# Two 64-row fp32 up-projections of a recurrence rewritten as hi/lo split products over 128 rows

## The chip, the cores and the metric

The kernel runs on one core of a Trainium2 chip. The metric is the device time of one execution in microseconds, the median of several runs. A core has a matrix engine (PE, whose weight loads are shown as PEld), a vector engine (DVE), an activation engine (ACT), a general engine (POOL), and DMA queues, of which this kernel issues nearly all from SP. Each engine works through its own list of instructions in order, and semaphores tie the lists together.

## The reference, cut to what matters

One decoder layer at SEQ 1024, D_MODEL 1024: a projection of the normed input, two token mixers beside each other (a recurrence called RWKV-7 and a state-space model called S5), an output projection, and a squared-ReLU MLP. The change touches the decay `w` and the gate `a` of the recurrence, each of which comes from a 64-column low-rank projection:

```python
r, k, v, wd, ad, gd = jnp.split(zm, [W, 2*W, 3*W, 3*W + 64, 3*W + 64 + 64], axis=-1)   # W = 512
w = jnp.exp(-DECAY_SCALE * jax.nn.sigmoid((w0 + jnp.tanh(wd) @ w_decay_up).astype(f32)))  # (64 -> 512)
a = jax.nn.sigmoid(a0 + ad @ w_aaa_up)                                                     # (64 -> 512)
```

Both products contract over 64. `w` and `a` then feed the recurrent state of 8 heads of 64.

## The kernel before, in words

Everything is held transposed: 128 features on the partitions, 512 tokens (one half `h` of the sequence) along the row. Products over weights are done in "split" form: a float32 tensor is written as hi + lo, both in the reduced type fp32r (hi by an ACT copy, lo by a DVE subtraction), and three products replace one, hi x hi, hi x lo and lo x hi (`mmacc`, lines 163 to 165). These are the *split products*; the page prints their operands as f32 too, and they are known by their lines. All other products (lines 183, 176, 549, 550, 588, 606 to 760) take plain float32 operands on PE.

The input projection makes 128 columns (`ct`) at a time: `load_w` brings and splits the weights, `mmacc` does 24 split products into a PSUM tile `mm` (two buffers), `zmix` scales by `rs` (the inverse norm, only known after `x_norm`) and mixes with the shifted tokens. Column 12 holds `wd` and `ad` one above the other; `z_lora` (line 307) makes it for each half into the tile `la`, with a tanh on the upper 64 rows. Column 13 (`sg`) is the gate.

The recurrence is cut into four rounds of two *units* (a unit is a pair of heads `hp` in a half `h`): `prep` (line 537, run 8 times) loads the unit's columns back from DRAM and calls the two products of this case, line 549 (`pw`, decay) from rows 0 to 63 of `lora` and `la`, and line 550 (`pa`) from rows 64 to 127. Each is a 64 x 128 weight against 64 x 512. Tile `swp` and tile `a` come from them. Then follow products within chunks of 64 tokens (`gram1`, `gram2`), a triangular inverse, a solve, and `sweep` (line 724): eight chunk steps, in each of which line 735 makes the next state `psn`, ACT writes it to `St` (lines 738, 123), and line 741 the output, for both units in turn. `post` ends the unit. S5 (`s5`) and the rest follow.

Up to the MLP the order of each engine's list is set by a scheduler that plays the program through with its own table of costs and takes what is ready by priority; the recurrence has high priority, and the input projection's split products fill in. From the MLP on the order is written by hand.

At the start, `raw` holds the eight 128 x 512 pieces of the input's first half in eight tiles that later steps use again: piece 3 is in the buffer tagged `kmod`, which `x_norm(1)` then uses for piece 3 of the second half, and `prep` for its tile `kmod`. `x_norm(h)` squares on ACT, adds into `xacc` on DVE, sums over partitions on PE (line 183, tile `stat`), scales on DVE (line 114, `statm`), takes the power on POOL, and goes by ACT and PE (line 176) into `rs`, without which no column can leave PSUM.

Of the kernel before, what the change touches and what calls it, by code (L numbers as in the profile page):

```python
# [9 lines left out]
F32 = mybir.dt.float32  # L10
F32R = mybir.dt.float32r
I32 = mybir.dt.int32
AF = mybir.ActivationFunctionType
# [61 lines left out]
def trunk(ctx, tc, A):  # L75
    nc = tc.nc
    PE, V, S, G, SY = nc.tensor, nc.vector, nc.scalar, nc.gpsimd, nc.sync

    def pool(name, bufs=1, space=None, c=None, **kw):
        if space is not None:  # L80
            kw["space"] = space
        return (c or ctx).enter_context(tc.tile_pool(name=name, bufs=bufs, **kw))
# [13 lines left out]
    def K(n):  # L96
        o, w = CST[n]
        return cst[:, o:o + w] if o < KEPT else cstw[:, o - KEPT:o - KEPT + w]

    def P(n, i):  # L100
        o, w = COL[n]
        return col[:, o + i:o + i + 1]
# [7 lines left out]
    def ts(e, out, in0, s1, op0, s2=None, op1=None):  # L110
        if op1 is None:
            e.tensor_scalar(out=out, in0=in0, scalar1=s1, scalar2=None, op0=op0)
        else:
            e.tensor_scalar(out=out, in0=in0, scalar1=s1, scalar2=s2, op0=op0, op1=op1)  # L114

    def tt(out, a, b, op):
        V.tensor_tensor(out=out, in0=a, in1=b, op=op)  # L117

    def stt(out, a, s, b, op0, op1):
        V.scalar_tensor_tensor(out=out, in0=a, scalar=s, in1=b, op0=op0, op1=op1)  # L120

    def act(out, in_, f, **kw):
        S.activation(out=out, in_=in_, func=f, **kw)  # L123

    M_, A_, B_ = ALU.mult, ALU.add, ALU.subtract
# [41 lines left out]
    def mmtile(p, tag="mm"):  # L167
        return p.tile([128, 512], F32, tag=tag, name=tag)
# [37 lines left out]
    wz = pool("wz", 2)  # L206

    w2 = pool("w2", 2, None, win)
# [3 lines left out]
    w0 = pool("w0", 1, None, ready, side="right")  # L212
# [10 lines left out]
    def st(shape=(128, 512)):  # L223
        return ps_st.tile(list(shape), F32, tag="st", name="st")
# [59 lines left out]
    def zcol(ct, h):  # L284
        x = xg[h]
        w = early.pop(ct) if ct in early else load_w(A["w_in"][ct], 1024)
        p = sm() if ct in (12, 13) and h == 0 else mmtile(ps_mm)
        mmacc(p, w, 8, lambda k: x[k][:, 0], lambda k: x[k][:, 1])
        return p

    def zmix(ct, h, out, p=None):
        p = p or zcol(ct, h)
        if normed[0]:
            act(out, p, AF.Copy, scale=omu[:, ct:ct + 1])
            stt(out[:, 1:512], p[:, 0:511], P("mu", ct), out[:, 1:512], M_, A_)
            stt(out[:, 0:1], carry[:, ct:ct + 1], P("mu", ct), out[:, 0:1], M_, A_)
            return
        z = wz.tile([128, 513], F32, tag="z", name="z")
        tt(z[:, 1:513], p, rs[h], M_)
        G.memset(z[:, 0:1], 0.0)  # L300
        G.tensor_copy(out=carry[:, ct:ct + 1], in_=z[:, 512:513])
        act(out, z[:, 1:513], AF.Copy, scale=omu[:, ct:ct + 1])
        stt(out, z[:, 0:512], P("mu", ct), out, M_, A_)

    la, sg = {}, {}

    def z_lora(h):
        la[h] = w2.tile([128, 512], F32, tag="la", name="la")
        p12, p13 = (first.pop(0), first.pop(0)) if first else (None, None)
        zmix(12, h, la[h], p12)  # L310
        act(la[h][0:64], la[h][0:64], AF.Tanh)
        sg[h] = w2.tile([128, 512], F32, tag="sg", name="sg")
        zmix(13, h, sg[h], p13)
        act(sg[h], sg[h], AF.Tanh, scale=0.5)
        ts(V, sg[h], sg[h], 0.5, M_, 0.5, A_)
# [33 lines left out]
    x_norm(0, raw)  # L349
    cstw = w1.tile([128, NCST - KEPT], F32, name="cstw")  # L350
    SY.dma_start(out=cstw, in_=A["cst"][:, KEPT:NCST])
    lora = w0.tile([128, 512], F32, name="lora")
    SY.dma_start(out=lora, in_=A["lora"])
    wgate = w1.tile([128, 512], F32, name="wgate")
    SY.dma_start(out=wgate, in_=A["wgate"])

# [180 lines left out]
    def prep(hp, h, slot):  # L537
# [8 lines left out]
        cs = slice(hp * 128, hp * 128 + 128)  # L546
        B, abd, rbd, BK = Bt[slot], abds[slot], rbds[slot], BKs[slot]
        pw, pa = st(), st()
        PE.matmul(pw, lhsT=lora[0:64, cs], rhs=la[h][0:64], start=True, stop=True)
        PE.matmul(pa, lhsT=lora[64:128, cs], rhs=la[h][64:128], start=True, stop=True)  # L550
        G.memset(swp[:, :, 0:1], 0.0)
        act(swp[:, :, 1:65], c8(pw), AF.Tanh, scale=0.5, bias=hw0[:, hp:hp + 1])
        act(swp[:, :, 1:65], swp[:, :, 1:65], AF.Copy, scale=0.5, bias=0.5)
# [344 lines left out]
    def rw_open(i):  # L898
        pr, h = pairs[i]
        with tc.high_priority():  # L900
            units[i] = [prep(2 * pr + n, h, n) for n in range(2)]
# [21 lines left out]
    def zprep(h):  # L923
        if h:
            xg[h] = make_xg(h, s2)
        z_lora(h)
# [67 lines left out]
    for m in range(8):  # L994
        if m % 2 == 0:
            w = load_w(A["w_proj"][m // 2], 1024)
        for h in range(2):
            p = mmtile(ps2, "b")
# [19 lines left out]
    for m in range(8):  # L1018
        w = load_w(A["w_glu"][m], 1024)
        for h in range(2):  # L1020
            pa, pb = mmtile(ps2, "b"), mmtile(ps2, "b")
# [9 lines left out]
            hi, lo = t[:, 0], t[:, 1]  # L1031
# [92 lines left out]
    for i, m in enumerate((0, 4, 1, 5, 2, 6, 3, 7)):  # L1124
# [7 lines left out]
        for h in range(2):  # L1132
            x = xs[m][:, h]
            p = mmtile(ps2, "b")
# [193 lines left out]
    def norm_step(i):  # L1328
# [5 lines left out]
        if i == 6:  # L1334
# [6 lines left out]
            pair[1].take("P2")  # L1341

    prep(2)
    prep(3)
    prep(4)
    ahead, stats = 5, []
    for i, (j, n) in enumerate(steps):
        r, o = divmod(i, 14)
# [129 lines left out]
    lo, hi = (0, 256), (256, 512)  # L1478
# [82 lines left out]
```

## Time and profile before

| | |
|---|---|
| median of 3 runs | 1520.98 us (1516.17 to 1527.92) |
| the profiled execution, its own time | 1516.6 us |
| its span from the first to the last instruction | 1514.8 us |
| PE busy | 1487.8 us, 98% of the span |
| DVE busy, ACT busy | 1076.9 us (71%), 728.4 us (48%) |
| granted clock of PE | 0.997 of full speed (2.4 GHz) |

The profile has a page (engines, time slices, the chain of work that ended last, groups of instructions) and views of its trace: stretches of time, waits, a timeline, and all instructions of a tile. A matmul's printed duration includes the part that overlaps with the next one; what one costs in a row of them is the distance between starts.

### The profile page before, as it was taken

What the parts mean: (1) busy time and instruction counts of PE and PEld (TensorE: products, weight loads), DVE (VectorE), ACT (ScalarE), POOL (GpSimd) and SP (SyncE); (2) the same over time, 40 slices, a digit from 0 to 9 for tenths busy, and PEclk for the clock granted to TensorE, in tenths of its full rate; (3) what the DMA queues carried; (4) which work ended last, traced back from release to release, by engine and by line L of the source; (5) the groups of instructions that cost most, each with busy time, mean ns of one, the idle gap of its engine ahead of it and who ended that gap; (6) DMA issues with size and microseconds to landing.
All of it is one profiled execution on the core that took longest, in us unless ns stands there. A gap on an engine that the chain in (4) does not pass through costs nothing.

```text
span 1514.8 us, 22409 instructions
## 1 busy us (share of the span) xinstructions
PE 1487.8 (98%) x8056; PEld 1216.2 (80%) x8056; DVE 1076.9 (71%) x2119; ACT 728.4 (48%) x1260; POOL 79.9 (5%) x108
## 2 busy tenths in 40 slices
PE   7999999999999999999999999999999999999996
PEld 5788887878788877878888888888888788888885
DVE  8669768888558768764656667777777767777574
ACT  6654766756656453323444454444444543333441
POOL 3110001101002001000000000000000000000000
PEclk9999999999999999999999999999999999999999
DMA  7554533444423525574114424444444686455571
GB/s 240 180 158 142 162 93 113 124 125 134 132 79 102 186 63 158 165 248 141 56 56 141 172 84 160 153 153 147 158 151 180 240 296 224 161 190 182 189 250 56
DMA packets 137679, 232.74 MB, mean 154 GB/s; under 512 B 42528, under 2 KB 52896, under 8 KB 137568
## 3 DMA queue, kind: packets, MB, share of 16 engines
q1 hardware_dynamic: 135776, 225.02, 45.2%
q10 hardware_dynamic: 1152, 4.19, 0.8%
q0 software_dynamic: 640, 2.10, 0.6%
q8 instruction: 64, 1.05, 0.3%
q14 instruction: 47, 0.39, 0.1%
HBM read 167.16 MB, written 62.91 MB: 152 GB/s over the span
## 4 chain that ended last, share of the span: by engine, by line
PE 88%; DVE 4%; ACT 3%; DMA 2%; issue 2%; SPq 0%; POOL 0%; POOLq 0%; DVEq 0%; ACTq 0%
PE mm L165 7%; PE mm L163 7%; PE mm L164 7%; PE b L163 5%; PE b L165 5%; PE b L164 5%; PE b L1385 4%; PE b L1386 4%; PE b L1387 4%; PE mm L1116 4%; PE mm L1117 4%; PE mm L1118 4%; PE b L1116 2%; PE b L1117 2%; PE b L1118 2%; PE sm L721 2%
## 5 line engine op out<-in xcount | busy, mean ns | idle before, releaser
L163 PE MATMUL mm<-s,whi 128*128 128x512 f32 x528 | 212.5, 402 | 0.0
L165 PE MATMUL mm<-s,wlo 128*128 128x512 f32 x528 | 212.1, 402 | 0.0
L164 PE MATMUL mm<-s,whi 128*128 128x512 f32 x528 | 209.6, 397 | 0.0
L123 ACT ACTIVATE whi<-wraw 128x512 fp32r<-128x512 f32 x176 | 103.2, 624 | 150.9 <-PE mm L164 58.6
L117 DVE TENSOR_TENSOR wlo<-wraw,whi 128x512 fp32r<-128x512 f32 x176 | 116.6, 684 | 49.1 <-ACT whi L123 45.0
L123 ACT ACTIVATE gp<-s 128x512 fp32r<-128x512 f32 (+1 forms) x127 | 81.7, 653 | 119.3 <-DVE s L117 102.5
L117 DVE TENSOR_TENSOR gp<-s,gp 128x512 fp32r<-128x512 f32 (+1 forms) x127 | 91.3, 722 | 55.3 <-ACT gp L123 55.2
L165 PEld LDWEIGHTS mm<-s,wlo 128*128 128x128 f32 x528 | 99.3, 188 | 23.8 <-issue 4.0
L163 PEld LDWEIGHTS mm<-s,whi 128*128 128x128 f32 x528 | 99.3, 188 | 23.8 <-issue 4.1
L164 PEld LDWEIGHTS mm<-s,whi 128*128 128x128 f32 x528 | 99.3, 188 | 22.8 <-issue 3.6
L1385 PE MATMUL b<-gp 128*128 128x512 f32 (+1 forms) x272 | 103.5, 380 | 2.1 <-DVE row L117 2.1
L1386 PE MATMUL b<-gp 128*128 128x512 f32 (+1 forms) x272 | 103.0, 379 | 0.0
L1387 PE MATMUL b<-gp 128*128 128x512 f32 (+1 forms) x272 | 102.9, 378 | 0.0
L123 ACT ACTIVATE gp<-kx 128x1024 fp32r<-128x1024 f32 x40 | 42.4, 1060 | 120.6 <-DVE kx L117 76.8
L186 POOL TENSOR_TENSOR statm<-statm,cst 128x8 f32<-128x8 f32 (+2 forms) x23 | 36.3, 1581 | 1066.6 <-DVE statm L114 994.1
L117 DVE TENSOR_TENSOR gp<-kx,gp 128x1024 fp32r<-128x1024 f32 x40 | 49.0, 1225 | 54.5 <-ACT gp L123 54.5
L117 DVE TENSOR_TENSOR s<-s,s 128x512 f32<-128x512 f32 (+2 forms) x120 | 75.4, 650 | 5.0 <-ACT s L823 4.6
L1116 PE MATMUL mm<-kx,gp 128*128 128x512 f32 x192 | 74.8, 389 | 0.0
L1118 PE MATMUL mm<-kx,gp 128*128 128x512 f32 x192 | 74.7, 389 | 0.0
L1117 PE MATMUL mm<-kx,gp 128*128 128x512 f32 x192 | 74.7, 389 | 0.0
L123 ACT ACTIVATE row<-row 128x512 f32<-128x512 f32 x64 | 40.0, 627 | 55.4 <-DVE row L120 55.4
L1385 PEld LDWEIGHTS b<-gp 128*128 128x128 f32 x272 | 51.6, 190 | 12.0 <-DVE row L117 2.5
(355 smaller groups left out, 3579.6 us busy)
## 6 DMA issues: line engine op xcount, KB each, us to landing
wraw<-in_w_in SPq DMA_DIRECT2D x136, 256.0 KB
wblk<-in_w_dn SPq DMA_DIRECT2D x40, 512.0 KB
s<-in_w_up SPq DMA_DIRECT2D x32, 512.0 KB
traw<-tDT SPq DMA_DIRECT2D x32, 512.0 KB
tD<-row SPq DMA_DIRECT2D x48, 256.0 KB
tDT<-gp SPq DMA_DIRECT2D x42, 256.0 KB
xraw<-in_xT SPq DMA_DIRECT2D x32, 256.0 KB
gD<-gt SPq DMA_DIRECT2D x32, 256.0 KB
```

What stands on the lines that cost most here:

```text
L117: V.tensor_tensor(out=out, in0=a, in1=b, op=op)
L123: S.activation(out=out, in_=in_, func=f, **kw)
L163: PE.matmul(out, lhsT=hi[:, a], rhs=rhi(k), start=(k == 0), stop=False)
L164: PE.matmul(out, lhsT=hi[:, a], rhs=rlo(k), start=False, stop=False)
L165: PE.matmul(out, lhsT=lo[:, a], rhs=rhi(k), start=False, stop=(k == nk - 1))
L186: G.tensor_tensor(out=m, in0=m, in1=K("mhalf")[:, 0:nj * n].rearrange("p (a b) -> p a b", b=n), op=ALU.pow)
L1116: PE.matmul(p, lhsT=hi[:, a], rhs=bh, start=(first and k == 0), stop=False, skip_group_check=True)
L1117: PE.matmul(p, lhsT=hi[:, a], rhs=bl, start=False, stop=False, skip_group_check=True)
L1118: r = PE.matmul(p, lhsT=lo[:, a], rhs=bh, start=False, stop=(k == 3), skip_group_check=True)
L1385: PE.matmul(p, lhsT=wh[:, a], rhs=th[:, c], start=first, stop=False, skip_group_check=True)
L1386: PE.matmul(p, lhsT=wh[:, a], rhs=tl[:, c], start=False, stop=False, skip_group_check=True)
L1387: PE.matmul(p, lhsT=wl[:, a], rhs=th[:, c], start=False, stop=stop, skip_group_check=True)
```

## The change

The tile `la` becomes two tiles of 128 rows, `dw` and `da`, each with hi on the 64 rows where the value stood and lo on the other 64. The weight tile `lora` becomes four tiles, `dwhi`, `dwlo`, `dahi`, `dalo`: the hi tile has hi of the weight on both halves, the lo tile has lo of the weight on the half of hi and zeros on the other. Two split products then give hi x (hi + lo) and lo x hi. So 16 products become 32 of another type. The weights' raw tile `lraw` takes the buffer tagged `kmod`, and the input's raw tile `lain` one of the two buffers tagged `zo`, through which all columns of `z_hp` pass.

```diff
     def z_lora(h):
-        la[h] = w2.tile([128, 512], F32, tag="la", name="la")
         p12, p13 = (first.pop(0), first.pop(0)) if first else (None, None)
-        zmix(12, h, la[h], p12)
-        act(la[h][0:64], la[h][0:64], AF.Tanh)
+        x = wz.tile([128, 512], F32, tag="zo", name="lain")
+        zmix(12, h, x, p12)
+        act(x[0:64], x[0:64], AF.Tanh)
+        dw, da = [w2.tile([128, 512], F32R, tag=n, name=n) for n in ("dw", "da")]
+        act(dw[0:64], x[0:64], AF.Copy)
+        act(da[64:128], x[64:128], AF.Copy)
+        tt(dw[64:128], x[0:64], dw[0:64].bitcast(F32), B_)
+        tt(da[0:64], x[64:128], da[64:128].bitcast(F32), B_)
+        la[h] = dw, da
...
-    lora = w0.tile([128, 512], F32, name="lora")
-    SY.dma_start(out=lora, in_=A["lora"])
+    lraw = w0.tile([128, 512], F32, tag="kmod", name="lraw")
+    SY.dma_start(out=lraw, in_=A["lora"])
+    lora = {}
+    for n, q, o in (("dw", slice(0, 64), slice(64, 128)), ("da", slice(64, 128), slice(0, 64))):
+        hi, lo = [w0.tile([128, 512], F32R, name=f"{n}{x}") for x in ("hi", "lo")]
+        act(hi[q], lraw[q], AF.Copy)
+        act(hi[o], lraw[q], AF.Copy)
+        act(lo[o], K("ones")[o].to_broadcast([64, 512]), AF.Copy, scale=0.0)
+        tt(lo[q], lraw[q], hi[q].bitcast(F32), B_)
+        lora[n] = hi, lo
...
-        PE.matmul(pw, lhsT=lora[0:64, cs], rhs=la[h][0:64], start=True, stop=True)
-        PE.matmul(pa, lhsT=lora[64:128, cs], rhs=la[h][64:128], start=True, stop=True)
+        for p, n, x in ((pw, "dw", la[h][0]), (pa, "da", la[h][1])):
+            hi, lo = lora[n]
+            PE.matmul(p, lhsT=hi[:, cs], rhs=x, start=True, stop=False)
+            PE.matmul(p, lhsT=lo[:, cs], rhs=x, start=False, stop=True)
```

The new products are lines 567 and 568 of the changed kernel; lines behind `prep` are 18 higher there (735 is 753). The scheduler deals all lists anew up to the MLP.

On PE, the second half's first unit. In the list before, its two products stand alone among the split products of the input projection (`mm`):

```order
L163 MATMUL mm<-s_2604,whi 128x512
L549 MATMUL st<-la,lora 128x512
L164 MATMUL mm<-s_2604,whi 128x512
L165 MATMUL mm<-s_2604,wlo 128x512
L163 MATMUL mm<-s_2562,whi 128x512
L164 MATMUL mm<-s_2562,whi 128x512
L550 MATMUL st<-la,lora 128x512
L165 MATMUL mm<-s_2562,wlo 128x512
```

In the list of the change the second of the two pairs of that unit:

```order
L163 MATMUL mm<-s_2612,whi 128x512
L164 MATMUL mm<-s_2612,whi 128x512
L165 MATMUL mm<-s_2612,wlo 128x512
L567 MATMUL st<-da,dahi 128x512
L568 MATMUL st<-da,dalo 128x512
L163 MATMUL mm<-s_2618,whi 128x512
```

Two plain float32 products among split ones have become neighbours of their own type. In the whole list before, lines 549 and 550 follow each other directly in one unit of eight; in the other seven, other products stand between them. Counted over PE's whole list, it changes between split and plain products 291 times before and 251 times with the change.

On DVE, from 20 us on, in the list before (`statm` is the norm of the first half, `z` the first columns to leave PSUM):

```order
L117 TENSOR_TENSOR xacc<-xacc,xraw 128x512 x4
L117 TENSOR_TENSOR wlo<-wraw,whi 128x512
L117 TENSOR_TENSOR xacc<-xacc,xraw 128x512 x2
L114 TENSOR_SCALAR statm<-stat 128x4
```

and in the list of the change:

```order
L117 TENSOR_TENSOR xacc<-xacc,xraw 128x512 x4
L117 TENSOR_TENSOR wlo<-wraw,whi 128x512
L117 TENSOR_TENSOR dwlo<-lraw,dwhi 64x512
L117 TENSOR_TENSOR dalo<-lraw,dahi 64x512
L114 TENSOR_SCALAR statm<-stat 128x4
```

The two subtractions for the new weight tiles stand ahead of the norm's scaling; on ACT the four copies `dwhi`, `dahi` that they read stand directly behind a weight's hi copy.

On PE, in the first sweep (`St` states, `Bt` one matrix per unit, told apart by its number). Before, behind two state products and one output product the input projection goes on:

```order
L606 MATMUL st<-BK_408,abd_406 128x128 x4
L735 MATMUL sm<-St,Bt_419 64x64 x2
L735 MATMUL sm<-St,Bt_416 64x64 x2
L741 MATMUL sm<-Bt_416,St 64x64 x2
L163 MATMUL mm<-s_2574,whi 128x512
```

With the change:

```order
L624 MATMUL st<-BK_420,abd_418 128x128 x4
L753 MATMUL sm<-St,Bt_431 64x64 x2
L753 MATMUL sm<-St,Bt_428 64x64 x2
L759 MATMUL sm<-Bt_428,St 64x64 x2
L753 MATMUL sm<-St,Bt_431 64x64
L759 MATMUL sm<-Bt_431,St 64x64
L753 MATMUL sm<-St,Bt_431 64x64
L759 MATMUL sm<-Bt_431,St 64x64
L753 MATMUL sm<-St,Bt_428 64x64
L759 MATMUL sm<-Bt_428,St 64x64
L753 MATMUL sm<-St,Bt_428 64x64
L759 MATMUL sm<-Bt_428,St 64x64
```

Four state products of the two units now follow each other with no split product between them. It is the only such run in either list; elsewhere at most two stand together.

## Rows read from the trace of the kernel before

**Rows 1.** The page: span, and busy time of each engine.
```profile
span 1514.8 us, 22409 instructions
PE 1487.8 (98%) x8056; PEld 1216.2 (80%) x8056; DVE 1076.9 (71%) x2119; ACT 728.4 (48%) x1260; POOL 79.9 (5%) x108
```

**Rows 2.** Stretches of time: the columns are in the first line.
```profile
core 0: us, PE busy (x) PEld busy (x) DVE busy (x) ACT busy (x) POOL busy (x), PEclk, DMA share, GB/s
0.00:20.00 20.00, 11.26 (x32) 7.10 (x33) 16.76 (x31) 14.50 (x26) 10.43 (x21) 1.00 0.87 298
20.00:30.00 10.00, 10.00 (x49) 8.40 (x48) 8.36 (x14) 5.74 (x11) 1.07 (x2) 1.00 0.62 207
30.00:37.00 7.00, 7.00 (x39) 5.61 (x37) 5.00 (x9) 5.20 (x9) 2.16 (x6) 1.00 0.50 152
...
200.00:300.00 100.00, 98.88 (x673) 79.26 (x672) 75.32 (x273) 70.08 (x143) 9.09 (x14) 1.00 0.40 122
...
400.00:500.00 100.00, 98.20 (x697) 79.48 (x696) 65.81 (x192) 63.67 (x132) 10.62 (x6) 1.00 0.38 112
```

**Rows 3.** PE's waits from 37 to 700 us: total, times, longest.
```profile
PE st L629 <- ACT Bt L642: 0.9, 1, 0.9
PE sm L710 <- ACT Bt L705: 0.9, 1, 0.9
PE sm L715 <- DVE Bt L117: 0.7, 2, 0.5
```

**Rows 4.** Tile `lora`: its products; two records make one product.
```profile
L549 PE MATMUL st<-la,lora x16: 589/641/693, 37.0 to 402.9; 64*128 64x512 f32 x16
L550 PE MATMUL st<-la,lora x16: 589/641/693, 37.0 to 408.6; 64*128 64x512 f32 x16
```

**Rows 5.** Timeline of PE, second half's first unit: start, duration.
```profile
259.44 0.39 PE L165 MATMUL mm<-s,wlo 128*128 128x512 f32 x1
259.67 0.39 PE L163 MATMUL mm<-s,whi 128*128 128x512 f32 x1
259.99 1.12 PE L549 MATMUL st<-la,lora 64*128 64x512 f32 x2
261.04 0.50 PE L164 MATMUL mm<-s,whi 128*128 128x512 f32 x1
261.37 0.39 PE L165 MATMUL mm<-s,wlo 128*128 128x512 f32 x1
261.60 0.40 PE L163 MATMUL mm<-s,whi 128*128 128x512 f32 x1
```

**Rows 6.** Timeline, first unit: both products directly behind each other.
```profile
36.99 0.69 PE L549 MATMUL st<-la,lora 64*128 64x512 f32 x1
37.00 0.69 PE L550 MATMUL st<-la,lora 64*128 64x512 f32 x1
38.05 0.50 PE L163 MATMUL mm<-s,whi 128*128 128x512 f32 x1
```

**Rows 7.** Timeline from 22 us: weights, the norm, a 64-row ACT write.
```profile
22.76 0.63 ACT L123 ACTIVATE whi<-wraw 128x512 fp32r<-128x512 f32 x1 [1.11 <-DMA wraw<-in_w_in]
24.63 0.16 DVE L114 TENSOR_SCALAR statm<-stat 128x4 f32<-128x4 f32 x1
31.88 1.28 DVE L117 TENSOR_TENSOR z<-sm,rs 128x512 f32<-128x512 f32 x2
34.22 0.64 ACT L123 ACTIVATE la<-la 64x512 f32<-64x512 f32 x1 [0.28 <-DVE la L120]
```

**Rows 8.** Timeline of the first sweep: a state product, and its write by ACT.
```profile
201.02 0.45 PE L735 MATMUL sm<-St,Bt 128*64 128x64 f32 x8
203.28 1.25 ACT L583 COPY BK<-a 64x512 f32<-64x512 f32 x2
204.56 1.31 ACT L123 ACTIVATE St<-sm,WC 64x64 f32<-64x64 f32 x4
```

## The prediction, made before the changed kernel had run

> **What bounds the kernel now.** I read the page first: PE is busy for 98% of the span, DVE for 71%, ACT for 48% [rows 1]. Since a mean can hide stages, I then read the stretches of time [rows 2]. PE is idle for 8.7 us of the first 20 us, and from 20 us on it is full: 10.00 of 10 and 7.00 of 7 us while the input's norm is made, 98.9 of 100 in the densest part of the recurrence, with ACT at 70% and DVE at 75% beside it. The third view is the list of PE's waits from 37 to 700 us: the longest is 0.9 us, and the three largest entries make 2.5 us [rows 3]. So in the stage of the change what ends last is PE's own list. The recurrence is a chain of small steps, but whenever one is late PE has split products of the input projection to do; a microsecond less work on PE is a microsecond of the span, as long as that filling lasts and the lists stay as well interleaved. That is the basis of the sum, and the place where it can break.
>
> **What PE saves.** Sixteen products of 64 rows go, 16 records on each of two lines and two records to a product [rows 4]. Where one stands alone it holds PE from 259.99 to 261.04, 1.05 us [rows 5]. Where the two are neighbours they start together at 36.99 and 37.00 and the next product starts at 38.05, 1.06 us for both [rows 6]. They are neighbours in one unit of eight, so PE gives them 1.06 + 14 x 1.05 = 15.8 us. Added are 32 split products of 128 rows; between split products starts are 259.44 and 259.67, 0.23 us apart [rows 5], so 32 x 0.23 = 7.4 us. The difference is **-8.4 us**.
>
> The trace's pair in [rows 6] shows two 64-row products overlapping entirely. The Trainium skill (TensorE: Matmul & The Clock Gate, "Part 3: Packing small matmuls — row/col tiling") makes this a rule: matmuls of few rows that lie in different row groups run concurrently, which speaks against widening them to 128 rows. By that rule in all eight units the old products would have cost 8 x 1.06 = 8.5 us and the change would save only 1.1; the trace agrees for the one unit whose products are neighbours, and the starts of the other seven units, 1.05 us for each product, decide for 8.4.
>
> **Changes of kind.** From a split product to a lone 64-row one the start comes 0.32 us later instead of 0.23 (259.67 to 259.99), and the first split product behind it takes 0.33 instead of 0.23 (261.04 to 261.37) [rows 5]: 0.1 us for each change of kind. PE's list changes kind 291 times before and 251 times after. That most of these 40 lie at other plain products, for which no row here has the price, leaves between 0 and 40 x 0.1 = 4.0 us. I take 3, near the row, **-3 us**.
>
> **What is added beside PE.** ACT gets ten writes of 64 rows: six for the weights, two in each half. The nearest row, a 64 x 512 tanh, has 0.64 us [rows 7]: 6.4 us. DVE gets six subtractions of 64 rows; the nearest row has two 128 x 512 operations in 1.28 us [rows 7], so at most 6 x 0.64 = 3.8 us. ACT has 4.3 us free of the 10 from 20 us on, and DVE 1.6 [rows 2]. PE's split products cover them; without that cover they would cost up to the 6.4 us of the longer engine.
>
> They are not covered where they stand ahead of the norm. DVE works in order, and `statm` now stands behind `dalo`, which needs all four ACT copies, which stand behind a weight copy that began at 22.76 [rows 7]: 22.76 + 0.63 + 4 x 0.64 = 25.95, plus 0.64 for `dalo`, so `statm` starts near 26.6 instead of 24.63, 2.0 us later, if the weights' DMA has come by then. Behind it are the power on POOL, `rs`, and the first columns to leave PSUM (31.88 before), and on them waits the third `mm` tile, as there are two buffers. The lone pair at 37 us no longer stands ahead of that tile; the scheduler has put split products there. Between 0 and 2 us, I take **+1**.
>
> DMAs: the weights' load is one of the same size as before. It is only moved on SP's queue, behind input pieces and a weight load, and waits until piece 3 of the input has been added up, since it takes that buffer; piece 3 of the second half waits for the splits in its turn. Who waits for that is the second half's `rs`, first used by the second half's columns near 200 us: more than 100 us of cover. `lain` holds one of two `zo` buffers a little longer; its cover is again PE's filling.
>
> In the second half the two ACT writes and two subtractions, 1.3 us on each engine, stand in the chain from column 12 to the decay, where ACT and DVE are at 70 and 75% [rows 2]. Between 0 and 2.6 us; with PE's waits so short I take **+0.5**.
>
> The bare run of the first sweep: before, the state product issued at 201.02 was written by ACT only from 204.56, 3.5 us later, because ACT had copies to finish [rows 8]; PE did split products meanwhile. In the changed list four state products follow each other, so PE must wait there for ACT. Between 0 (ACT free) and twice 3.5 us; ACT's list now has the state writes behind four such copies instead of eight, so less than one whole wait: **+1.5**. Late next are then the columns behind it, whose split products simply follow.
>
> **Sum.** -8.4 - 3 + 1 + 0.5 + 1.5 = -8.4 us. Against the profiled execution's own 1516.6 us (1514.8 of span and 1.8 around it) this is 1508.2. The median of the runs, 1520.98, lies 4.4 us above the profiled one, which is near the fastest; from the median the same sum gives 1512.6. I forecast the middle, **1510 us**.
>
> **The rivals.**
>
> *All of it is kept (0.16).* The norm and the sweep lose nothing, the changes of kind count in full, and the 2.5 us of waits [rows 3] fall away in the new lists: -8.4 - 4.0 - 2.5 = -14.9, 1502 to 1506 from the two bases. For it: PE full from 20 us on [rows 2]. Against it: the later `statm` and the bare run stand in the lists.
>
> *No gain (0.14).* PE's freed time turns into waits, because its busy time is not its limit and the chain through ACT and DVE, at 70 and 75% in the recurrence [rows 2], ends last there. The price is the whole gain: 1517 to 1523. Against it: with equal filling those waits would already show, and they are 2.5 us in 663 [rows 3]. The Trainium skill (Trainium Kernel Development and Optimization, "Performance Expectations") supports the doubt: matmul busy time is a bad metric for a distance to the limit, weight-load busy time a good one. The weight loads here are at 80% [rows 1], which by that rule would leave room; the starts 0.23 us apart without a gap [rows 5] say there is little.
>
> *Slower (0.10).* The new lists expose the state chain. One sweep has eight steps; if each ends in a 3.5 us wait for ACT's write [rows 8] with no split product between, that is 28 us, and 28 - 11.4 = +16.6, 1533 to 1538. It decides from four bare waits on (4 x 3.5 = 14 against 11.4 saved). For it: the first sweep now has a bare run, and the first unit's products stand 33 split products (7.6 us) later in PE's list. Against it: it is the only bare run.
>
> That the new products don't run as split products, but at 1.05 us each (32 x 1.05 - 15.8 = +17.8), can hardly be: [rows 5] has the same shape and type. I give it nothing of its own.
>
> **How the numbers follow.** The forecast has 0.60, with 1504 to 1517 as its own range: the bounds of its terms are -12.4 (nothing given back, all 4.0 kept) and +3.2 (no change of kind counts, 2 + 2.6 + 7 given back), which few runs should reach at once. From 1501 to 1523 the range holds the forecast, most of the first rival and the second; left out are the slower one and 0.08 at the edges. About 1% is what a measurement of this kernel can tell from no change: the bounds are 1505.8 and 1536.2. Faster: 0.12 of the first rival and 0.10 of the forecast's lower end, 0.22. Slower: 0.06 of the third rival. Same: the remaining 0.72.
>
> **What would show it.** The new lines at 0.46 us a pair from start to start, and PE's time for them near 7.4 us; the split-to-plain changes at 0.1 us; `statm` near 26.6 us and the third `mm` tile not over 2 us late; one wait on ACT's `St` write of up to 3.5 us near the first sweep; PE's waits from 37 to 700 us at 3 to 8 us in sum. From the MLP on the lists are the same and everything should only lie some 8 us earlier. Wrong would make it: waits of PE above 12 us in sum, a PE busy time that falls by less than 8 us, or a start that loses more than 3 us.

## The result, and the profile after

The changed kernel takes 1535.0 us (median of 21 executions, 1525.86 to 1546.75) against 1523.08 of the kernel before on the same chip; the ratio is 1.0082 with an interval of 1.0066 to 1.0098. It is slower by 0.8%, above the predicted range. The profiled execution took 1530.3 us. From the page of the changed kernel, the lines that answer to [rows 1]:

```profile
span 1528.5 us, 22423 instructions
PE 1494.0 (98%) x8056; PEld 1232.2 (81%) x8056; DVE 1083.3 (71%) x2125; ACT 733.4 (48%) x1270; POOL 73.5 (5%) x108
```

PE's share looks the same, yet its busy time grew by 6.2 us although it has less to do. The stretches of [rows 2], in the changed kernel, show why:

```profile
0.00:20.00 20.00, 11.00 (x31) 7.16 (x32) 16.31 (x31) 15.31 (x27) 10.45 (x21) 1.00 0.84 283
20.00:30.00 10.00, 10.00 (x49) 8.38 (x48) 7.31 (x13) 8.42 (x16) 1.50 (x2) 1.00 0.74 237
200.00:300.00 100.00, 97.24 (x655) 80.54 (x653) 76.02 (x257) 68.91 (x138) 8.34 (x13) 1.00 0.43 133
400.00:500.00 100.00, 96.63 (x636) 81.00 (x635) 58.72 (x166) 56.57 (x120) 5.24 (x6) 0.88 0.33 101
```

The start is as before to 0.3 us. In the recurrence PE now has more idle time (busy for 97.24 and 96.63 us of 100, instead of 98.88 and 98.20), and from 400 to 500 us its granted clock is 0.88 instead of 1.00. PE's waits from 37 to 700 us in the changed kernel, to be laid beside [rows 3]:

```profile
PE sm L739 <- ACT Bt L734: 3.4, 1, 3.4
PE sm L733 <- DVE Bt L117: 1.9, 1, 1.9
PE sm L753 <- ACT St L123: 1.6, 1, 1.6
PE sm L837 <- ACT s L829: 1.3, 1, 1.3
PE st L567 <- ACT swp L123: 1.2, 1, 1.2
PE mm L163 <- ACT whi L123: 1.1, 1, 1.1
PE st L624 <- DVE vb L117: 0.3, 1, 0.3
```

These seven make 10.8 us; the whole list before made 3.8. The longest is read in the timelines of PE and ACT (start, duration, instruction, in brackets the idle time ahead of it and what ended it):

```profile
415.54 1.05 PE L733 MATMUL sm<-Bt,Tbd 128*128 128x128 f32 x8
419.97 0.58 PE L739 MATMUL sm<-Bt,AL 64*128 64x128 f32 x1 [3.37 <-ACT Bt L734]
```

```profile
414.98 0.63 ACT L123 ACTIVATE swp<-swp 128x512 f32<-128x512 f32 x1
418.72 0.72 ACT L123 ACTIVATE sq<-km,col 128x512 f32<-128x512 f32 x1 [3.11 <-DMA km<-zDkm]
419.35 0.57 ACT L734 COPY Bt<-sm 128x512 f32<-128x512 f32 x1
```

PE needs the copy of `Bt`. ACT could have made it soon after 415.6, but works in order, and ahead of it stands a square of the next unit's keys, which waits 3.11 us for a DMA. In the kernel before the square also stands ahead of the copy, but it waited 0.32 us for its load, and five other ACT instructions stood between the two. Then the clock, in stretches of 5 us of the changed kernel (the granted clock is the third number from the end):

```profile
415.00:420.00 5.00, 1.63 (x14) 1.36 (x12) 1.24 (x1) 1.89 (x4) 0.00 (x0) 0.99 0.37 105
420.00:425.00 5.00, 5.00 (x19) 4.28 (x19) 1.29 (x2) 4.33 (x9) 0.00 (x0) 0.50 0.00 0
435.00:440.00 5.00, 5.00 (x23) 3.48 (x23) 4.42 (x8) 0.62 (x2) 0.00 (x0) 0.50 0.00 0
440.00:445.00 5.00, 5.00 (x20) 3.83 (x21) 2.49 (x4) 2.75 (x5) 0.00 (x0) 0.62 0.04 14
```

The clock falls at 419.9, at the end of the wait, and PE runs at 1.2 GHz until 443.7, through the small products of the solve and the sweep; it rises after a run of split products. By the granted clock 11.9 us of full speed are missing in these 25 us, more than three times the wait. The whole span has a granted clock of 0.987, against 0.997 before.

**Time goes with the clock.** Each execution comes with its granted clock. Over 329 executions of all kernels here, lines of one slope, with a height for each kernel, leave a scatter of 1.3 us; the slope is 1.34 us for each 0.001 of clock. The kernel before has two groups, near 0.997 (1516 us, a third of its executions) and near 0.991 (1524 us, most others); the changed one has 0.974 to 0.989. The last column of the table moves all to 0.997 by that slope (interval of the mean in brackets). The kernels from x_hold on are explained in the next section. One of x_fill's ten executions, 1544.0 us, counts as slow and is left out of its ratio.

| kernel | median us | ratio to before, interval | median clock | at 0.997 |
|---|---|---|---|---|
| before | 1523.2 (146 executions) | | 0.992 | 1516.0 (0.2) |
| changed | 1535.0 | 1.0082, 1.0066 to 1.0098 | 0.983 | 1516.0 (0.8) |
| x_hold | 1524.85 | 1.0033, 1.0009 to 1.0057 | 0.990 | 1514.7 (0.7) |
| x_swap | 1538.55 | 1.0135, 1.0088 to 1.0182 | 0.9845 | 1522.5 (1.6) |
| x_hi | 1523.65 | 1.0013, 0.9986 to 1.0041 | 0.989 | 1513.5 (1.1) |
| x_pad | 1524.62 | 1.0020, 1.0001 to 1.0039 | 0.9915 | 1518.0 (0.9) |
| x_add | 1523.51 | 0.9994, 0.9974 to 1.0014 | 0.992 | 1516.6 (0.9) |
| x_fill | 1531.09 | 1.0042, 1.0015 to 1.0069 | 0.9865 | 1516.6 (0.9) |
| e_sq2 | 1526.45 | 1.0041, 1.0014 to 1.0068 | 0.990 | 1516.8 (1.1) |
| b_sq2 | 1527.26 | 1.0031, 1.0007 to 1.0055 | 0.991 | 1519.9 (0.5) |
| x_dense | 1549.45 | 1.0175, 1.0159 to 1.0190 | 0.986 | 1534.9 (1.1) |
| b_stat | 1514.98 | 0.9956, 0.9932 to 0.9980 | 0.996 | 1514.5 (0.6) |
| b_stat2 | 1514.53 | 0.9958, 0.9938 to 0.9978 | 0.996 | 1514.2 (0.8) |
| x_stat | 1519.85 | 0.9978, 0.9951 to 1.0005 | 0.991 | 1511.8 (0.7) |
| x_best | 1523.57 | 0.9992, 0.9967 to 1.0017 | 0.9905 | 1515.9 (0.7) |
| x_pad1 | 1517.67 | 0.9971, 0.9946 to 0.9996 | 0.9945 | 1513.9 (0.6) |
| a_stat | 1523.32 | 1.0006, 0.9986 to 1.0025 | 0.989 | 1512.7 (1.2) |
| a_best | 1524.92 | 1.0023, 1.0002 to 1.0044 | 0.989 | 1512.7 (0.9) |

The kernels ran on several chips; each ratio is to the kernel before on the same chip, whose own median went from 1520.9 to 1523.7 us, so medians of different kernels that lie 2 us apart say little. The brackets leave out the error of the slope: the lines of single kernels with ten or more executions have slopes from 1.0 (a_best) to 1.9 (b_stat2). Differences of 1 to 3 us in the last column between kernels whose clocks lie far apart are estimates.

At the same clock the changed kernel and the kernel before are equal by this estimate. In sum all of the loss is clock: the mean is 0.0099 lower, 13 us. That does not say that nothing else changed; x_swap below shows a gain and a loss at the same clock that cancel.

### The profile page after: what moved, and what is told of

Read it like the earlier page. It is cut to its first block, busy times and chain, and to the rows that moved or that the text cites. A ratio compares the mean times of both kernels' runs of the same rounds, so it can differ in the third digit from the quotient of the medians.

```text
span 1528.5 us, 22423 instructions
## 1 busy us (share of the span) xinstructions
PE 1494.0 (98%) x8056; PEld 1232.2 (81%) x8056; DVE 1083.3 (71%) x2125; ACT 733.4 (48%) x1270; POOL 73.5 (5%) x108
## 3 DMA queue, kind: packets, MB, share of 16 engines
q8 instruction: 64, 1.05, 0.3%
## 4 chain that ended last, share of the span: by engine, by line
PE 89%; DVE 4%; DMA 4%; ACT 2%; issue 2%; SPq 1%; POOLq 0%; POOL 0%; DVEq 0%; ACTq 0%
PE mm L163 7%; PE mm L165 7%; PE mm L164 7%; PE b L163 5%; PE b L164 5%; PE b L165 5%; PE b L1403 4%; PE mm L1135 4%; PE mm L1134 4%; PE b L1404 4%; PE b L1405 4%; PE mm L1136 4%; PE sm L739 2%; PE b L1134 2%; PE b L1135 2%; PE b L1136 2%
## 5 line engine op out<-in xcount | busy, mean ns | idle before, releaser
L186 POOL TENSOR_TENSOR statm<-statm,cst 128x8 f32<-128x8 f32 (+2 forms) x23 | 35.0, 1524 | 1033.4 <-DVE statm L114 996.7
L1403 PEld LDWEIGHTS b<-gp 128*128 128x128 f32 x272 | 51.2, 188 | 11.9 <-DVE row L117 2.5
```

The costliest lines, as they stand in the source:

```text
L186: G.tensor_tensor(out=m, in0=m, in1=K("mhalf")[:, 0:nj * n].rearrange("p (a b) -> p a b", b=n), op=ALU.pow)
L1403: PE.matmul(p, lhsT=wh[:, a], rhs=th[:, c], start=first, stop=False, skip_group_check=True)
```

## The experiments

The theory after the first comparison, T, was that the products save what was worked out and that the new order of the lists, through PE's waits and the clock behind them, makes the loss; R1 that the wider products and their ACT and DVE work make it; R2 that the clock falls for another reason. W, C and S come from later runs: W, that PE's freed time turns into waits; C and S, that the clock falls where PE runs small products, S naming one alternation of them near 190 us. All kernels here except e_sq2 and b_sq2 have *held* lists: at the end of the kernel's code each instruction is tied to the one that shall stand ahead of it on its engine, so that the scheduler keeps a given order.

```diff
+        for p, q in zip(seq, seq[1:]):
+            tc.add_manual_dep(q, p.name, free, reason="hold")
```

**The products, or the order? (x_hold, x_swap.)** x_hold has the new products in the old lists. So that no buffer forces another order, `lain` and `lraw` get a buffer of their own.

```diff
-        x = wz.tile([128, 512], F32, tag="zo", name="lain")
+        x = w2.tile([128, 512], F32, tag="la", bufs=1, name="lain")
```

> The changed computation with every engine's list held in the order of the kernel before; only the 16 + 10 + 6 added instructions are put in, the second product of each pair right behind the first, the four of the first unit nine places later. Theory T (the products themselves save what was worked out, and the loss is made by the new order of the lists): 1511 to 1516 us where the kernel before has 1521 to 1523, the granted clock at 0.996 or more, PE's waits from 37 to 700 us below 6 us in sum. Rival R1 (the wider products, or the ACT and DVE work that comes with them, cost the time whatever the order): no faster than the kernel before, 1523 to 1540 us, clock below 0.990.

x_swap has the old products in the new lists (the kernel before and a held order, no other edit).

> The mirror image: the old products (64 rows, plain) with every engine's list held in the order of the changed kernel, the added instructions left out. T: the order alone makes the loss, so the long wait of PE near 416 us and the half clock behind it are there with the old products too: 1532 to 1545 us, granted clock 0.980 to 0.990. R1: as the kernel before, 1517 to 1526 us, clock 0.996 or more.

x_swap is slower than the kernel before by 1.35%: the new order alone does it, and R1 cannot say why. But its own trace has no wait of more than 1.9 us from 37 to 700 us; the lists run a little differently with the old products, and the long wait near 416 us was not there. And T missed in x_hold, whose median and clock lie in R1's range: at the same clock 1.3 us are won (3 by x_hold's own slope), not 8.4, and the clock is lower, with one of 12 executions at 0.994 or more where the kernel before had 14 of 29 on the same chip. In its trace it falls at 186.2, behind a wait of 1.05 us. So R1 may hold in part: with the order held, the new products seem to bring the clock down too. x_hold's waits from 37 to 700 us make 12.4 us, the longest entries being

```profile
PE sm L733 <- DVE Bt L117: 3.2, 3, 1.5
PE sm L722 <- DMA Tbd<-TD: 2.7, 3, 2.0
PE sm L728 <- ACT Bt L723: 2.2, 2, 1.5
```

Where the gain went can be seen at one unit. The kernel before, and then x_hold, on PE around the gate's product:

```profile
408.07 1.12 PE L550 MATMUL st<-la,lora 64*128 64x512 f32 x2
410.13 1.16 PE L710 MATMUL sm<-Bt,LO 128*128 128x128 f32 x8 [0.94 <-ACT Bt L705]
```

```profile
416.76 0.48 PE L567 MATMUL st<-da,dahi 128*128 128x512 f32 x1
417.08 0.39 PE L568 MATMUL st<-da,dalo 128*128 128x512 f32 x1
418.99 1.16 PE L728 MATMUL sm<-Bt,LO 128*128 128x128 f32 x8 [1.52 <-ACT Bt L723]
```

From the product's start PE is busy for 0.71 us instead of 1.12 until the wait begins, and the wait is 0.58 us longer. What PE no longer does there, it waits. So a theory W took T's place: PE waits for ACT and DVE at the next step of the recurrence, and the old products were part of what filled that time.

**How much is PE's time worth? (x_hi, x_pad.)** Both change x_hold's PE work alone.

In x_hi:

```diff
-            PE.matmul(p, lhsT=hi[:, cs], rhs=x, start=True, stop=False)
-            PE.matmul(p, lhsT=lo[:, cs], rhs=x, start=False, stop=True)
+            PE.matmul(p, lhsT=hi[:, cs], rhs=x, start=True, stop=True)
```

In x_pad:

```diff
+            for _ in range(3):
+                PE.matmul(p, lhsT=hi[:, cs], rhs=x, start=True, stop=True)
             PE.matmul(p, lhsT=hi[:, cs], rhs=x, start=True, stop=False)
```

> x_hold without the second product of each pair (the low part of the weight is left out of the computation): 16 split products less, 3.7 us of PE work. Theory W (PE waits for ACT and DVE at the next step, so what PE saves is not won): within 1.5 us of x_hold at the same granted clock, median 1522 to 1527 us, PE's waits from 37 to 700 us 2 to 4 us longer in sum than in x_hold. Rival (PE's list ends last): 3.7 us less than x_hold at the same clock, median near 1521 us, waits as in x_hold.

> x_hold (the changed computation in the lists of the kernel before) with three split products that nobody needs ahead of each of the 16 pairs, so that PE has about as much to do there as with the old products: 48 x 0.23 = 11 us of PE work more. Theory W (after x_hold: the PE time that the new products free is not won, because PE then waits for ACT and DVE at the next step of the recurrence): the added work goes into those waits, 1522 to 1529 us, at most 4 us more than x_hold at the same granted clock, PE's waits from 37 to 700 us 5 to 8 us instead of 12. Rival (PE's own list ends last, as the prediction had it): 11 us more than x_hold, 1534 to 1538 us, the waits unchanged.

With 3.7 us less work the waits in x_hi grow to 16.0 us, by 3.6; with 11 us more they fall to 8.0. The three profiles lie at different clocks (x_hi 0.996, x_hold 0.989, x_pad 0.991), which may move the waits too. At the same clock the times are 1513.5, 1514.7 and 1518.0: 3.7 us of work bring 1.2, not clear of noise, and 11 us cost 3.3. A microsecond of PE here is worth about 0.3 us, by each kernel's own slope up to 0.6, and not 1. W holds. From the medians x_pad, with 11 us of useless products, is no slower than x_hold: its clock is a little better.

**The added ACT and DVE work (x_add).**

```diff
+        act(dw[0:64], x[0:64], AF.Copy)
+        act(da[64:128], x[64:128], AF.Copy)
+        tt(dw[64:128], x[0:64], dw[0:64].bitcast(F32), B_)
```

(and the like for the weights; the old products read none of it).

> The kernel before in its own lists, with the 10 ACT writes and 6 DVE subtractions of the change put in at the places that they have in x_hold; what they write is not used, and the products are the old ones. T and W: the added work is hidden, 1519 to 1525 us, clock spread as in the kernel before (0.990 to 0.997). R1 (this work costs the time): 1528 us or more.

It is 0.9994 of the kernel before. R1's second half, the added ACT and DVE work, falls; the work is hidden.

**The long wait (x_fill, e_sq2).** x_fill holds the changed kernel's lists and puts products into the wait; e_sq2 changes one rule and lets the scheduler deal.

In x_fill, for one unit, `fill` 16:

```diff
+            for _ in range(fill):
+                PE.matmul(w.rearrange("p a b -> p (a b)"), lhsT=lora["dw"][0][:, 0:128], rhs=la[1][0],
+                          start=True, stop=True)
```

In e_sq2 (`last_px` is the last copy of the solve):

```diff
+            if i in (2,):
+                tc.add_manual_dep(units[i + 1][1].sq, last_px[0].name, mybir.DependencyInfo(
+                    mybir.DependencyClass.NoSync, mybir.DependencyReason.DATA), reason="order")
```

> The changed kernel, all lists held in its own order, and 16 split products that nobody needs (0.23 us each, 3.7 us) put where PE waits 3.4 us near 416 us. T: PE does not stand idle there, so the stretch behind it keeps 2.4 GHz: about 12 us less than the changed kernel (23 us at half the clock are 11.9 us of loss), 1521 to 1526 us, clock about 0.994. Rival R2 (the clock falls for another reason than that wait): the same stretch at half the clock, 1530 to 1540 us, clock about 0.987.

> The changed kernel with one rule of order more: in the third round ACT's square of the second unit's keys is queued behind the last copy of the solve, so that the copy does not stand behind a DMA. The scheduler deals the lists with that rule. T: no wait over 2 us near 416 us and no half clock there: 1516 to 1525 us, clock 0.992 or more. R1 and R2: 1530 to 1540 us.

Filling the wait brings 3.9 us in the medians, where T expected 12, and x_fill's median lies in R2's range. The mean clock rises from 0.983 to 0.9877, and two of ten executions reach 0.996, which none of the changed kernel's 21 does. So that wait is part of the cause, and less than one profile made it seem. x_fill's trace is of the slowest of its executions, 1544.0 us at 0.977. The wait is filled there, PE is busy without a pause from 428.7 us on, and the clock falls all the same at 440.6, where 64-row products alternate with products of two columns:

```profile
433.82 3.98 PE L184 MATMUL stat<-dw,dwhi 128*128 128x512 f32 x16
437.50:440.00 2.50, 2.50 (x17) 2.00 (x16) 1.03 (x2) 2.44 (x5) 0.00 (x0) 1.00 0.00 0
440.00:442.50 2.50, 2.50 (x13) 2.12 (x14) 0.42 (x2) 0.00 (x0) 0.32 (x1) 0.62 0.00 0
```

e_sq2 comes to 1526.45, 1.5 us above its range; its profile has the fall at 420 us no more, but one at 191.7 us, where PE had not waited since 172 us.

**Is any new deal a change? (b_sq2.)** The rule of e_sq2 in the kernel before.

> The kernel before with the one rule of order of e_sq2, nothing else changed: the scheduler deals anew what stands behind that point (662 of 6816 places in PE's list differ). Theory T (a new deal alone moves waits and clock): the time differs from the kernel before by 3 us or more in either direction, with waits of over 1 us that the kernel before has not. Rival (a deal with so small a change is worth nothing): within 2 us of the kernel before.

The same computation, with several hundred of the 6816 places of PE's list different, is 1.0031 of the kernel before, 3.9 us more at the same clock. The order of the lists alone moves the time by about half of what this change was to bring.

**The fall near 190 us (x_dense, b_stat, x_stat).** In the profiles of x_hold, x_pad, e_sq2 and x_dense (below) the clock falls between 185 and 193 us. What PE does there, in x_pad, where it had not waited from 171 us on:

```profile
183.56 1.95 PE L735 MATMUL sm<-Bt,Tbd 128*128 128x128 f32 x16
185.44 0.48 PE L741 MATMUL sm<-Bt,AL 64*128 64x128 f32 x2
185.85 0.38 PE L183 MATMUL stat<-cst,sq 128*128 128x2 f32 x2
186.16 0.49 PE L741 MATMUL sm<-Bt,AL 64*128 64x128 f32 x2
186.58 0.38 PE L183 MATMUL stat<-cst,sq 128*128 128x2 f32 x2
...
187.62 0.48 PE L741 MATMUL sm<-Bt,AL 64*128 64x128 f32 x2
188.04 0.38 PE L183 MATMUL stat<-cst,sq 128*128 128x2 f32 x2
```

Products of 64 rows alternate with products of two columns. In x_pad the clock falls at 188.3, at the end of that alternation, and in e_sq2 at 191.7, 1.3 us behind it. The kernel before has the alternation too, and its profiled execution, one of those near 0.997, keeps the full clock there:

```profile
185.00:190.00 5.00, 5.00 (x41) 4.42 (x40) 3.55 (x8) 3.48 (x8) 1.17 (x2) 1.00 0.43 134
```

So the fall is not in every execution, and for the kernel before no trace shows one. x_dense puts split products ahead of each group; b_stat and x_stat put the two-column products together in two rounds, as they stand in the other six of the eight units.

In x_dense, with `fill` 2 in the first three rounds:

```diff
+                for _ in range(fill):
+                    PE.matmul(po.rearrange("p a b -> p (a b)"), lhsT=lora["dw"][0][:, 0:128], rhs=lora["dw"][0],
+                              start=True, stop=True)
```

PE's list in the first round of b_stat:

```diff
 L715 MATMUL sm<-Bt1,Tbd1
+L183 MATMUL stat<-cst,sq
+L183 MATMUL stat<-cst,sq
+L183 MATMUL stat<-cst,sq
+L183 MATMUL stat<-cst,sq
 L721 MATMUL sm<-Bt0,AL
-L183 MATMUL stat<-cst,sq
 L721 MATMUL sm<-Bt0,AL
-L183 MATMUL stat<-cst,sq
 L721 MATMUL sm<-Bt0,AL
-L183 MATMUL stat<-cst,sq
 L721 MATMUL sm<-Bt0,AL
-L183 MATMUL stat<-cst,sq
```

> x_hold with two split products that nobody needs ahead of each of the eight groups of 64 x 128 products that end the solve, in the first three rounds: 48, 11 us of PE work. Theory C (the half clock comes where PE runs these small products with few split products between them, with or without a wait): the granted clock is 0.994 or more in nearly all executions, no stretch of half clock from 180 to 460 us, and 1521 to 1528 us with a narrow spread. Rival (the half clock comes from waits alone, or by chance): clock near 0.990 as in x_hold, 1532 to 1538 us.

> The kernel before in its own lists, with one move on PE: in the first and the third round the four two-column products of the key's norm (line 183), which lie one by one between the first products of 64 rows of the solve, stand together ahead of them (first round) or at the place of the first of them (third round), as they do in the other six units. No wait of PE is near that place before. Theory S (the half clock near 190 us, in most executions of most kernels here, comes from that thin stretch): the granted clock is 0.996 or more in nearly all executions, median 1514 to 1518 us. Rival (it comes by chance or from waits elsewhere): as before, two thirds of the executions at 0.990 to 0.992, median 1520 to 1524 us.

> x_hold with the same move as in b_stat. S: the fall near 185 us goes, median 1514 to 1519 us, clock 0.994 or more in most executions. Rival: as x_hold, 1523 to 1527 us.

x_dense misses what C expected: its clock is 0.985 to 0.987, and it fell at 185.5, again in the alternation, which stands ahead of most of the added products and has none inside. It cost 20 us more than x_hold at the same clock, 11 of them the products; the rest is not settled.

b_stat confirms S: 11 of 12 executions have 0.996 or more (the kernel before: a third), and it is 0.44% faster than the kernel before by a move of two groups of four small products. Which of the two groups does it was not tried. x_stat gained 5 us against x_hold, but misses S's range: two of 12 executions are at 0.994 or more, and the clock still falls, without the alternation. First x_stat, then x_pad1 (below), in stretches of 5 us.

```profile
180.00:185.00 5.00, 5.00 (x46) 4.89 (x46) 5.00 (x9) 5.00 (x12) 0.12 (x1) 1.00 0.61 199
185.00:190.00 5.00, 4.46 (x22) 3.61 (x21) 3.68 (x7) 2.86 (x6) 1.64 (x1) 0.58 0.33 92
190.00:195.00 5.00, 5.00 (x22) 4.06 (x22) 0.69 (x1) 0.35 (x1) 0.00 (x0) 0.50 0.01 3
```

```profile
180.00:185.00 5.00, 5.00 (x44) 4.75 (x43) 5.00 (x8) 5.00 (x11) 0.12 (x1) 1.00 0.58 191
185.00:190.00 5.00, 4.97 (x36) 3.95 (x34) 3.77 (x8) 2.85 (x6) 1.64 (x1) 1.00 0.26 82
190.00:195.00 5.00, 5.00 (x46) 3.86 (x46) 3.94 (x7) 0.74 (x3) 0.00 (x0) 1.00 0.00 0
```

In x_stat PE waits 0.54 us until 185.9, and the clock falls in that wait; if the shorter products have brought PE there too early, useless ones ahead of it should take the wait away.

**Filling that wait (x_best, x_pad1).** x_best moves seven split products from ahead of the solve into it; x_pad1 adds three useless ones ahead of each of the two pairs of one unit, at 172 and 180 us:

```diff
+            for _ in range(3 if (h, hp) == (0, 3) else 0):
+                PE.matmul(p, lhsT=hi[:, cs], rhs=x, start=True, stop=True)
```

> x_stat, in which seven of the 21 split products that stand ahead of the first round's second solve pass are moved behind its first eight 64 x 128 products, three ahead of the second and four ahead of the third group (where PE waited 0.5 us). No product is added. Theory S with waits (the clock falls near 185 us in x_stat because that wait makes the thin stretch thinner): no fall there in most executions, median 1511 to 1516 us, clock 0.995 or more, faster than both kernels. Rival: as x_stat, 1518 to 1522 us, clock 0.991.

> x_stat with six split products that nobody needs (1.4 us of PE work), three ahead of each pair of the one unit whose products lie at 172 and 180 us, ahead of the thin stretch; they give PE there the time that the old products took. Theory S with waits (in x_stat the freed time becomes a wait inside the thin stretch, and the clock falls on it): the wait near 186 us is gone and so is the fall, clock 0.995 or more in most executions, median 1511 to 1516 us, 4 to 8 us faster with more work. Rival: as x_stat or slower by the added work, 1520 to 1522 us, clock 0.991.

x_best is a miss. Its moved products leave 1.6 us less cover ahead, and in its trace PE waits 0.60 us for ACT's `sq` at 183.28 instead; the clock falls at 185.2, where x_stat's falls at 185.8. Five of its 12 executions hold 0.996, but at the same clock it is 4 us slower than x_stat. x_pad1 does more work than x_stat and holds the clock better: 11 of 12 executions are at 0.994 or more, against 2 of 12, and the wait is gone. Its median is 2.2 us lower, but on another chip, and the ratios to the kernel before (0.9971 and 0.9978) do not tell the two apart. The median, 1517.67, is above the expected 1511 to 1516; a short fall that loses 1.7 us, behind a wait of 1.66 us for DVE at 295.37, is left in its trace.

**Back to the changed kernel (a_stat, a_best, b_stat2).** a_stat makes b_stat's move in the changed kernel's own lists, there in three rounds, and nothing else; a_best also moves ACT's square behind two copies, and the products that need it behind those that do not.

ACT's list in a_best:

```diff
-L123 ACTIVATE sq<-km
 L734 COPY Bt<-sm
 L123 ACTIVATE Wp<-swp
 L734 COPY Bt<-sm
 L123 ACTIVATE swp<-swp
 L580 COPY WC<-Wp
 L123 ACTIVATE a<-st
+L123 ACTIVATE sq<-km
 L734 COPY Bt<-sm
```

> The changed kernel in its own lists, with the move of b_stat: in the first three rounds the four two-column products of the key's norm stand together ahead of the 64-row products of the solve. The long wait near 416 us stays. Theory S (its low clock is made of falls at thin stretches, the one near 190 us among them, and of the wait near 416): one fall less in most executions, mean clock 0.987 to 0.991 instead of 0.983, median 1524 to 1531 us. Rival (the falls come by chance, or from the wider products): as the changed kernel, clock near 0.983, median 1533 to 1537 us.

> a_stat, and in the third round ACT's square of the second unit's keys stands behind the first two copies of the solve's second pass (it waits for a DMA there), and on PE the four two-column products that read it, and the four that spread the result, behind the 64-row products that do not need it. No work is added or left out. Theory S with waits (what is left of the low clock in a_stat is the fall at 420 us behind the wait for that copy): no wait over 2 us and no fall there, clock 0.994 or more in most executions, median 1512 to 1518 us, faster than the kernel before and the changed one. Rival: as a_stat, 1521 to 1525 us, clock 0.989.

> b_stat once more, on the chip of a_best: the old products with the clock held. If what a_stat and x_stat show is right (at the same granted clock the new products save 2 to 3 us against b_stat), a_best lies 0 to 4 us below it where both hold the clock. Rival (the products save nothing): a_best at b_stat or above it. b_stat itself: 1514 to 1517 us.

a_stat takes 11.7 us off the changed kernel, all that it had lost, by the place of three groups of four small products. The mean clock rises by 0.0059, worth 8 us; the other 3 us are won at the same clock. Its executions lie at 0.987 to 0.990, and a fall is still in its trace, at 421.5, behind a wait of 2.21 us for ACT's square. a_best has two waits of 0.47 and 1.14 us there, and that is no gain. On PE:

```profile
415.59 1.16 PE L739 MATMUL sm<-Bt,AL 64*128 64x128 f32 x8 [0.47 <-ACT Bt L734]
417.89 4.28 PE L739 MATMUL sm<-Bt,AL 64*128 64x128 f32 x24 [1.14 <-ACT Bt L734]
```

The clock falls at 417.8, at the end of the second. So the waits that are left there, or the run of small products itself, may do as much as the long wait; this stays open. b_stat repeats: 1514.53. At the same clock x_stat (1511.8), in b_stat's own lists, lies 2.6 us below b_stat and b_stat2 (1514.4), and a_stat (1512.7), in other lists, 1.7 us: by this estimate that is what the new products are worth when the order is mended. No version with them kept the clock as b_stat does, and b_stat, with the old products, is the fastest kernel here; it beats both.

## Why the prediction was wrong

**The products: size right, worth wrong.** The new lines start 0.23 us apart, with no change of kind between them:

```profile
45.22 0.48 PE L165 MATMUL mm<-s,wlo 128*128 128x512 f32 x1
45.54 0.39 PE L567 MATMUL st<-dw,dwhi 128*128 128x512 f32 x1
45.77 0.40 PE L568 MATMUL st<-dw,dwlo 128*128 128x512 f32 x1
46.01 0.39 PE L567 MATMUL st<-da,dahi 128*128 128x512 f32 x1
46.24 0.39 PE L568 MATMUL st<-da,dalo 128*128 128x512 f32 x1
46.47 0.40 PE L163 MATMUL mm<-s,whi 128*128 128x512 f32 x1
```

In the same lists (the changed kernel against x_swap, equal changes of kind, clocks near each other) they save 6.4 us at the same clock, with an interval of some 2 us, near the 8.4 of the sum; in the old lists 1.3 to 3.

**The step that failed** is the basis: "a microsecond less work on PE is a microsecond of the span, as long as that filling lasts and the lists stay as well interleaved". Neither held. In the old lists a microsecond was worth about 0.3, because waits that are short do not mean that PE is the limit: they were short since the old products filled them. And the lists did not stay: in the new deal 2875 of 6816 places of PE's list hold another product (x_swap against the kernel before), and it costs some 6.5 us at the same clock even with the old products. PE's waits grew from 3.8 to 10.8 us where 3 to 8 was expected, and PE's busy time, which was to fall by 8 us or more, rose by 6.2. Which waits make up the 6.5 us is not settled.

**The term that was missing** is the clock. [Rows 2] have 1.00 in every stretch, and the sum took that as given. The spread of the runs shown, 1516 to 1528 us, was taken as noise to be split in the middle; it is the clock of the kernel before, which is lower in two thirds of its executions. With it goes all of the measured loss: 9.9 x 1.34 = 13 us, and at the same clock 0, the 6.4 us of the products and the 6.5 of the order cancelling. That the order brings the clock down is shown by x_swap and a_stat; what makes it fall in one execution and not in another stays open.

**Steps that held.** `statm` starts at 25.07, 0.4 us later where 2.0 was worked out and +1 taken: ACT's copies for `dwhi` start at 21.0, ahead of the weight copy that the estimate put before them, and `statm` waits 0.38 us for PE's `stat`, not for `dalo`. The bare sweep run costs 1.57 us:

```profile
202.43 0.33 PE L753 MATMUL sm<-St,Bt 128*64 128x64 f32 x2 [1.57 <-ACT St L123]
```

1.5 was taken. The added ACT and DVE work is hidden, as x_add shows. The 0.1 us for a change of kind were not tested by themselves; the 251 changes belong to the new lists, x_swap has them with the old products and is no faster, so nothing shows the 3 us that the sum took for them.

**The rivals.** "No gain" named the first mechanism, PE's time turned into waits behind ACT and DVE, and had 0.14; x_hi and x_pad show it. "Slower" named the wrong wait: the state chain cost one wait of 1.6 us, not eight of 3.5, and the long one was for a copy behind a DMA. No rival named the clock. Of what was cited, the Trainium skill (Trainium Kernel Development and Optimization, "Performance Expectations"), which calls matmul busy time a bad metric, was the better guide: matmul busy time, 98% in both, told nothing. The Trainium skill (TensorE: Matmul & The Clock Gate, "HAM oscillation — how this bites in real kernels") also tells of matmuls that run at the lower clock behind waits for data; the stretch behind 419.97 agrees, and the fall at 188.3 in x_pad, with no wait behind 171 us, is not of that kind.

## What to carry to other kernels

A full engine with short waits is a list that was dealt to be full: before a saving on it is booked, ask what stands behind the freed time, and test the worth of a microsecond by adding useless work. Compare executions at the same granted clock, and look for the clock in the spread of the runs: one profile shows one execution. A change that makes a scheduler deal anew is two changes; hold the lists to tell them apart.

## What was not expected of the hardware

- One wait of 3.37 us was followed by 24 us at 1.2 GHz, though PE was busy for all of it (5.00 of 5 us in each stretch from 420 to 440): 11.9 us of full speed missing by the granted clock, of which filling the wait brought back 3.9 in the medians.
- The clock also falls where PE does not wait: at 188.3 us in x_pad and 191.7 in e_sq2, at the end of an alternation of 64-row and two-column products and just behind it. Putting the two-column products together in two rounds raised the share of executions at 0.994 or more from 51 of 146 to 22 of 24 (b_stat, b_stat2).
- Six useless products raised the share of executions at 0.994 or more from 2 of 12 to 11 of 12 (x_pad1 against x_stat), at no cost in time.
